# Features of the next even pair of heads beside the substitution of the recurrence

## The chip, the cores and the metric

One core of one Trainium2 chip runs the whole kernel as one launch. The metric is the device time in microseconds. The engines are named as in the profile: PE (TensorE), DVE (VectorE), ACT (ScalarE), POOL (GpSimd) and SP, whose queue issues the DMAs. PEld is TensorE's weight load.

## The reference

One layer of a diffusion backbone over 256 latent tokens with 256 context tokens, model width 2048, all in float32. The part that matters here is the RWKV-7 mixing: 16 heads of 64 channels, and for each head two recurrences over 512 tokens (context, then latent), one forward and one backward:

```
def step(S, inp):
    r_t, w_t, k_t, v_t, kk_t, a_t = inp
    sa = jnp.einsum('bhvk,bhk->bhv', S, kk_t)
    S = (S * w_t[:, :, None, :] - sa[..., None] * (kk_t * a_t)[:, :, None, :]
         + v_t[..., None] * k_t[:, :, None, :])
    return S, jnp.einsum('bhvk,bhk->bhv', S, r_t)
...
out = (y.reshape(B_, L, C) * g).astype(p.dtype)
```

Around it stand adaLN with RMSNorm, one input projection (2048 to 10880 columns), differential attention, a gated merge of both mixers (`sigmoid(p_gate)`, `w_pa`, `w_pb`, `w_out`) and a mixture of 32 experts, of which two work on each token.

## The kernel before

The recurrence is done in chunks of 64 tokens (8 chunks in each direction). A pair is two heads on 128 partitions; there are eight pairs, and a round `q` (0 to 3) works on an even and an odd pair, `2q` and `2q + 1`. A round consists of these steps, all traced by generators:

- `feat` (line 1015), once for each pair: loads k, v, r and, for each direction, two low-rank weights and two rows of `lora`; makes the decays, their scan (line 1062), the scaled keys `kq` (lines 1089 and 1091) in the places b0 and b1 for the even pair and b2 and b3 for the odd one, the queries R, and last the bonus `bon` with a product on TensorE (line 1103). GpSimd does lines 1068, 1078 to 1081, 1095 and 1099.
- `within` (line 1109), once for each pair: the products of keys and queries in each chunk, pc and px, the masked blocks A and M, the diagonal blocks `dg16` in the place "s" of the pool `rb`, and transposed keys `kt`.
- `inverse` (line 1406): unit triangular 64x64 blocks are inverted. Their 32x32 diagonal blocks go by substitution on DVE: `na` by a transposition, then 31 steps of a product (line 1422) and a sum (line 1424), each on blocks that grow by one, then two transpositions, ZT and Z (lines 1427 and 1429). The rest of the blocks follows by 32x32 products on TensorE, ph and pz (lines 1438 and 1447): the blocked end.
- `deltas` (line 1193): first `inverse` with `side` pulled along (transposes of P and v, and `values`), then the products with the inverse, pW and pu, then G and the chain of states over the chunks (line 1333), and the outputs py. The features of the next round's two pairs are traced here, by `ahead(n)` after each step.
- `tail`: normalises and gates a round's output. It is braided with the next round's `within` of the odd pair.

While these run, `interleave` gives credit for each yielded number to a stream of background steps: projections with weights that arrive by DMA into eight `raw` tiles, are split into a high and a low part (ACT casts `whi`, line 964, and `wlo` is a subtraction, line 965), and feed 12 or 24 matmuls (line 486). While `self.low` is set, in the substitution, the subtraction is on GpSimd instead of DVE. The order on each engine is set by the tile scheduler: it takes the ready instruction that is traced first, by a model of durations, and hands out the places of a tag in the order of the trace. Instructions that are traced later may stand earlier if they are ready and their place is free; on the chip each engine then goes in that fixed order. After the four rounds come the merge and the experts, whose weights (403 MB) are streamed.

Of the kernel before, what the change touches and what calls it, by code (L numbers as in the profile page):

```python
# [9 lines left out]
F32 = mybir.dt.float32  # L10
# [8 lines left out]
P = 128  # L19
# [181 lines left out]
class Body:  # L201
# [793 lines left out]
    def feats(self, q):  # L995
        self.ce = self.rwt("ce", [P, 2, 2, NC], 2)

        self.vv = self.rwt("vv", [P, NC, 2, C])
        self.pts = [self.rwt(f"P{d}", [P, NC, 2, C]) for d in range(2)]
        a = yield from self.feat(2 * q)  # L1000
        b = yield from self.feat(2 * q + 1)
        return a, b

# [189 lines left out]
    def deltas(self, st, q):  # L1193

        nc, K, pt = self.nc, self.K, self.pts
        pst, tl, ident = self.pst, self.rwt, self.ident
# [3 lines left out]
        def side():  # L1200
            for dc in range(0, 2 * NC, 4):
                pp = pst("pp")
                for c in range(4):
                    nc.tensor.transpose(pp[:, c * P:(c + 1) * P], pt[dc // NC][:, dc % NC + c].rearrange("p o t -> p (o t)"), ident)
                nc.scalar.copy(W[:, dc:dc + 4, :], pp.rearrange("p (c f) -> p c f", c=4))
                yield
            yield from self.values(st)

        side = side()
        self.low = nc.gpsimd  # L1210
        for n, w in enumerate(self.inverse([s["A"] for s in st])):
            if n % 2:
                next(side, None)
            yield w * (1.0 if q < 3 else 0.731)
        for _ in side:
            pass
        self.low = None

        fe, nxt = (self.feats(q + 1) if q < 3 else iter(())), [None]

        def ahead(n):
            for _ in range(n):
                try:
                    w = next(fe)
                except StopIteration as e:
                    if e.value is not None:
                        nxt[0] = e.value
                    return
                if isinstance(w, str):
                    yield w  # L1230

        for dc in range(0, 2 * NC, 4):
            d, c0 = dc // NC, dc % NC
# [22 lines left out]
        for i0, ni in ((0, 4), (4, 2)):  # L1256
            pg = [pst("pG") for _ in range(2)]
            for i in range(ni):
                for d, c in enumerate(order[i0 + i + 1]):
                    for h in range(2):  # L1260
                        for s in st:
                            o, us = s["o"], H2[1 - s["o"]]
                            n = (2 * i + d) * C
# [142 lines left out]
    def inverse(self, As):  # L1406

        nc, tl, pst = self.nc, self.rwt, self.pst
        NB = 2 * NC * 2
        Av = [A.rearrange("p d c h t -> p (d c h) t") for A in As]  # L1410

        na = tl("na", [P, 32, 32], tag="b0")
        z = tl("z", [P, 32, 32], tag="b1")
        prod = tl("prod", [P, 32, 32], tag="b2")
        rows = self.rows
        nc.vector.transpose(na.rearrange("b s t -> b t s"), self.dg16.rearrange("p d n t -> p t (d n)"))
        yield 1.5
        nc.gpsimd.memset(z, 0.0)
        nc.gpsimd.memset(z.rearrange("b s t -> b (s t)")[:, ::33], 1.0)
        for s in range(30, -1, -1):  # L1420
            n = 31 - s
            nc.vector.tensor_tensor(prod[:, :n, :n], z[:, s + 1:, s + 1:], na[:, s, s + 1:].unsqueeze(1).to_broadcast([P, n, n]),
                                    ALU.mult)
            nc.vector.tensor_reduce(z[:, s + 1:, s], prod[:, :n, :n], AX.X, ALU.add)
            yield 0.25 + n * n * 0.002
        ZT = H = tl("ZT", [P, NB, 32], tag="b3")
        nc.vector.transpose(ZT.rearrange("p n s -> p s n"), z.rearrange("b t s -> b s t"))
        Z = self.rb.tile([P, NB, 32], F32, tag="s", name="Z")
        nc.vector.transpose(Z.rearrange("p n t -> p t n"), z)
        yield 3.077  # L1430

        for g in range(2):
            ph = [pst("ph") for _ in range(2)]
            for o in range(2):
                r0, r1 = rows(o, 0), rows(o, 1)
                for n in range(16):
                    m = g * 16 + n
                    nc.tensor.matmul(ph[o][r1, n * 32:n * 32 + 32], Av[o][r0, m, 32:64], ZT[r0, m, :],
                                     start=True, stop=True, tile_position=(r0.start, r1.start))
                nc.scalar.copy(H[r1, g * 16:g * 16 + 16], ph[o][r1, :].rearrange("p (n t) -> p n t", n=16))  # L1440
            yield 0.7
            pz = [pst("pz") for _ in range(2)]
            for o in range(2):
                r0, r1 = rows(o, 0), rows(o, 1)
                for n in range(16):
                    m = g * 16 + n
                    nc.tensor.matmul(pz[o][r0, n * 32:n * 32 + 32], H[r1, m, :], Z[r1, m, :],  # L1447
                                     start=True, stop=True, tile_position=(r1.start, r0.start))
                nc.scalar.copy(Av[o][r0, g * 16:g * 16 + 16, 32:64], pz[o][r0, :].rearrange("p (n t) -> p n t", n=16))
                nc.scalar.copy(Av[o][rows(o, g), :, 32 * g:32 * g + 32], Z[rows(o, g)])  # L1450
            yield 0.7
# [518 lines left out]
```

## Time and profile before

| | us |
|---|---|
| median of three runs | 2506.11 |
| lowest, highest | 2496.79, 2522.02 |
| the profiled execution, span | 2507.6 |
| the same, with what lies around the span | 2509.57 |

The span runs from the first to the last instruction. Busy time of TensorE is modelled: a busy TensorE need not be at its peak. The granted clock is a mean over a stretch; 1.00 is 2.4 GHz and 0.50 is 1.2 GHz.

### The profile page before, as it was taken

Reading aid. Unit: us, or ns where it says so; the run is one execution under the profiler, and the core shown is the slowest. Engines: PE = TensorE matmul, PEld = TensorE weight load, DVE = VectorE, ACT = ScalarE, POOL = GpSimd, SP = SyncE. Lnnn points to the kernel's source line nnn. Section 1 sums busy time; section 2 is a strip of 40 time slices with the busy share of each in tenths; the row PEclk is TensorE's granted clock in tenths of the full one; section 3 lists DMA queues with packets and bytes.
Section 4 is the critical chain, followed back from the end, with each engine's and each line's share of the span. In section 5 each row is a group of like instructions: output and inputs, shape, how many; then the busy total and the mean of one; then the engine's idle time right before and its main releaser. Section 6 shows DMA issues by size and latency. Waiting matters only on the chain.

```text
span 2507.6 us, 45450 instructions
## 1 busy us (share of the span) xinstructions
PE 2346.5 (94%) x18419; PEld 1654.6 (66%) x18419; DVE 1204.9 (48%) x2239; ACT 796.6 (32%) x1479; POOL 219.7 (9%) x279
## 2 busy tenths in 40 slices
PE   6999989899999899999999898999999999999997
PEld 3799977788998687787899876444444434443442
DVE  3355677778655674766745654222222222222223
ACT  3332345455354655656534442000000000000000
POOL 0110012113113332102000000000000000000000
PEclk9999999999998998989889999999999999999999
DMA  9977764567754332353438897799999999999997
GB/s 348 340 243 242 238 204 138 168 206 242 231 156 124 106 115 77 122 163 100 132 116 253 257 322 273 319 421 421 420 421 421 420 421 421 421 421 421 421 421 323
DMA packets 233127, 691.50 MB, mean 276 GB/s; under 512 B 34840, under 2 KB 72400, under 8 KB 182864
## 3 DMA queue, kind: packets, MB, share of 16 engines
q1 hardware_dynamic: 232912, 688.54, 74.3%
q8 instruction: 146, 2.39, 0.4%
q14 instruction: 69, 0.57, 0.1%
HBM read 666.66 MB, written 21.78 MB: 275 GB/s over the span
## 4 chain that ended last, share of the span: by engine, by line
PE 50%; DMA 31%; DVE 8%; issue 5%; ACT 3%; POOL 2%; SPq 1%; DVEq 0%; ACTq 0%; POOLq 0%
DMA w<-in_exp_w_dram 17%; PE acc L486 12%; PE acc L517 6%; DMA r<-in_exp_w_dram 5%; PE pa L1821 5%; PE po L1856 4%; PE pt L1753 3%; PE acc L811 3%; DMA raw<-in_ws_dram 3%; DMA d<-in_exp_w_dram 2%; DVE wlo L965 1%; PE pc L1128 1%; PE ada L647 1%; PE pu L1247 1%; PE pz L1447 1%
## 5 line engine op out<-in xcount | busy, mean ns | idle before, releaser
L1821 PE MATMUL pa<-w,hg 128*64 128x512 f32 x1408 | 390.2, 596 | 35.0 <-DMA w<-in_exp_w_dram 31.8
L964 ACT CAST whi<-raw 128x512 fp32r<-128x512 f32 (+1 forms) x463 | 280.1, 614 | 310.7 <-PE acc L486 148.4
L965 DVE TENSOR_TENSOR wlo<-raw,whi 128x512 fp32r<-128x512 f32 (+1 forms) x420 | 289.4, 704 | 85.2 <-ACT whi L964 79.9
L1821 PEld LDWEIGHTS pa<-w,hg 128*64 128x64 f32 x1408 | 119.8, 137 | 245.5 <-issue 178.0
L486 PE MATMUL acc<-xr,whi 128*128 128x256 f32 (+1 forms) x1248 | 269.7, 294 | 0.7 <-ACT whi L964 0.7
L486 PE MATMUL acc<-xd,whi 128*128 128x256 f32 (+1 forms) x1248 | 267.2, 291 | 0.3 <-DVE g L750 0.2
L486 PEld LDWEIGHTS acc<-xr,whi 128*128 128x128 f32 (+1 forms) x1248 | 209.0, 195 | 20.0 <-issue 17.6
L486 PEld LDWEIGHTS acc<-xd,whi 128*128 128x128 f32 (+1 forms) x1248 | 206.3, 192 | 18.3 <-issue 14.1
L1768 DVE TENSOR_TENSOR hm<-hm,pa 128x512 f32<-128x512 f32 x16 | 11.0, 688 | 417.9 <-PE pa L1821 417.9
L1856 PE MATMUL po<-w,hT 128*64 128x512 f32 (+1 forms) x712 | 191.9, 587 | 1.6 <-DMA w<-in_exp_w_dram 0.9
L486 PE MATMUL acc<-xr,wlo 128*128 128x256 f32 (+1 forms) x624 | 182.7, 293 | 4.4 <-DVE wlo L965 3.9
L486 PE MATMUL acc<-xd,wlo 128*128 128x256 f32 (+1 forms) x624 | 181.5, 291 | 1.6 <-DVE wlo L965 1.6
L603 DVE SCALAR_TENSOR_TENSOR ada<-raw,cs,ada 128x512 f32<-128x512 f32 x180 | 136.8, 768 | 87.9 <-DMA raw<-in_ws_dram 87.6
L1875 DVE TENSOR_TENSOR acc<-acc,pt 128x512 f32<-128x512 f32 x112 | 75.3, 683 | 152.1 <-PE pt L1868 152.1
L1858 ACT ACTIVATE oh<-po,gc 128x512 fp32r<-128x512 f32 (+1 forms) x65 | 44.4, 683 | 314.9 <-PE po L1856 314.9
L1753 PE MATMUL pt<-pe,xa 128*128 128x128 f32 x1024 | 123.4, 279 | 5.9 <-DVE hg L1755 5.2
L486 PEld LDWEIGHTS acc<-xr,wlo 128*128 128x128 f32 (+1 forms) x624 | 121.5, 195 | 8.9 <-DVE wlo L965 5.7
L1753 PEld LDWEIGHTS pt<-pe,xa 128*128 128x128 f32 x1024 | 118.5, 194 | 12.1 <-DVE hg L1755 8.8
L486 PEld LDWEIGHTS acc<-xd,wlo 128*128 128x128 f32 (+1 forms) x624 | 119.7, 192 | 5.1 <-DVE wlo L965 2.4
L1856 PEld LDWEIGHTS po<-w,hT 128*64 128x64 f32 x712 | 57.6, 136 | 92.9 <-issue 87.5
L1821 PE MATMUL pa<-d,hg 128*64 128x512 f32 x304 | 109.2, 596 | 6.2 <-DMA d<-in_exp_w_dram 6.2
L1821 PE MATMUL pa<-r,hg 128*64 128x512 f32 x312 | 102.4, 596 | 7.9 <-DMA r<-in_exp_w_dram 7.9
(402 smaller groups left out, 4395.1 us busy)
## 6 DMA issues: line engine op xcount, KB each, us to landing
w<-in_exp_w_dram SPq DMA_DIRECT2D x263, 1024.0 KB
raw<-in_ws_dram SPq DMA_DIRECT2D x703, 256.0 KB
r<-in_exp_w_dram SPq DMA_DIRECT2D x58, 1024.0 KB
d<-in_exp_w_dram SPq DMA_DIRECT2D x58, 1024.0 KB
xt<-in_ws_dram SPq DMA_DIRECT2D x39, 512.0 KB
raw<-in_ws_dram SPq DMA_DIRECT2D x25, 512.0 KB
g<-gate SPq DMA_DIRECT2D x48, 128.0 KB
kvr<-own SPq DMA_DIRECT2D x16, 256.0 KB
```

The costliest lines, as they stand in the source:

```text
L486: m = nc.tensor.matmul(acc[j][:M, n * T:n * T + T], a[:, k2, j * M:(j + 1) * M], (rl if i == 1 else rh)[k], start=(k == 0 and i == 0 and s ...
L517: m = nc.tensor.matmul(acc[b][:, n * 256:n * 256 + 256], (ll if i == 2 else lh)[k][:, ts], (lo if i == 1 else hi)[:, k2, :], start=(k == 0 ...
L603: nc.vector.scalar_tensor_tensor(a, raw, c, a, ALU.mult, ALU.add)
L647: self.nc.tensor.matmul(bank[0][j, :], self.cs[:, k, :], raw[:, k - k0, :], start=(k < 4), stop=(k >= KT - 4), tile_position=(0, j.start))
L811: nc.tensor.matmul(acc[i], a[:, i * P:(i + 1) * P], b[:, k - k0, :], start=(k == 0 and q == 0), stop=(k == KT - 1 and q == 2))
L964: self.nc.scalar.copy(hi, src)
L965: (eng or self.nc.vector).tensor_tensor(lo, src, f32(hi), ALU.subtract)
L1753: nc.tensor.matmul(p[:, k * P:(k + 1) * P], xa[:, i, (k4 + k) * P:(k4 + k + 1) * P], pe[:, i, :], start=(i == 0), stop=(i == 1))
L1821: nc.tensor.matmul(a[es_, :], hg[:, k4 + k, es_], w[e][:, k, :], start=(k4 + k == 0), stop=(k4 + k == KT - 1), tile_position=(0, e * 64))
L1856: nc.tensor.matmul(o[es_, :], hT[:, f, es_], w[e][:, f, hs], start=(f == 0), stop=(f == 3), tile_position=(0, e * 64))
L1858: nc.scalar.activation(oh[:, n, hs], o, AF.Copy, scale=gc)
L1875: nc.vector.tensor_tensor(acc[:, i, os], acc[:, i, os], y, ALU.add)
```

## The change

Four edits. `feats` yields `False` between its two pairs. `deltas` makes the generator of the next features before the substitution, pulls `side` at each of its first twelve steps (then at every second), and from step 12 on pulls the features by one or two steps each time, but only as far as the end of the even pair; what is left of the even pair is traced behind the blocked end, and the odd pair is pulled in the deltas as before. `self.low` is reset behind that. In `inverse` the tiles take other places: `na` b2 (was b0), `prod` b3 (was b2), `z` the place "s" of the diagonal blocks (was b1), made after they are read, and `Z` b2 (was "s"). So b0 and b1 are free for the next even pair's keys during the substitution. In the last round there are no next features.

```
--- before.py
+++ after.py
@@ -998,6 +998,7 @@
         self.vv = self.rwt("vv", [P, NC, 2, C])
         self.pts = [self.rwt(f"P{d}", [P, NC, 2, C]) for d in range(2)]
         a = yield from self.feat(2 * q)
+        yield False
         b = yield from self.feat(2 * q + 1)
         return a, b
 
@@ -1206,28 +1207,37 @@
                 yield
             yield from self.values(st)
 
-        side = side()
-        self.low = nc.gpsimd
-        for n, w in enumerate(self.inverse([s["A"] for s in st])):
-            if n % 2:
-                next(side, None)
-            yield w * (1.0 if q < 3 else 0.731)
-        for _ in side:
-            pass
-        self.low = None
-
-        fe, nxt = (self.feats(q + 1) if q < 3 else iter(())), [None]
+
+        fe, nxt, even = (self.feats(q + 1) if q < 3 else iter(())), [None], [True]
 
         def ahead(n):
             for _ in range(n):
+                if even[0] is None:
+                    return
                 try:
                     w = next(fe)
                 except StopIteration as e:
                     if e.value is not None:
                         nxt[0] = e.value
                     return
+                if w is False and even[0]:
+                    even[0] = None
                 if isinstance(w, str):
                     yield w
+
+        side = side()
+        self.low = nc.gpsimd
+        for n, w in enumerate(self.inverse([s["A"] for s in st])):
+            if n < 12 or n % 2:
+                next(side, None)
+            if n >= 12:
+                yield from ahead(1 + n % 2)
+            yield w * (1.0 if q < 3 else 0.731)
+        for _ in side:
+            pass
+        yield from ahead(100)
+        even[0] = False
+        self.low = None
 
         for dc in range(0, 2 * NC, 4):
             d, c0 = dc // NC, dc % NC
@@ -1409,11 +1419,11 @@
         NB = 2 * NC * 2
         Av = [A.rearrange("p d c h t -> p (d c h) t") for A in As]
 
-        na = tl("na", [P, 32, 32], tag="b0")
-        z = tl("z", [P, 32, 32], tag="b1")
-        prod = tl("prod", [P, 32, 32], tag="b2")
+        na = tl("na", [P, 32, 32], tag="b2")
+        prod = tl("prod", [P, 32, 32], tag="b3")
         rows = self.rows
         nc.vector.transpose(na.rearrange("b s t -> b t s"), self.dg16.rearrange("p d n t -> p t (d n)"))
+        z = self.rb.tile([P, 32, 32], F32, tag="s", name="z")
         yield 1.5
         nc.gpsimd.memset(z, 0.0)
         nc.gpsimd.memset(z.rearrange("b s t -> b (s t)")[:, ::33], 1.0)
@@ -1425,7 +1435,7 @@
             yield 0.25 + n * n * 0.002
         ZT = H = tl("ZT", [P, NB, 32], tag="b3")
         nc.vector.transpose(ZT.rearrange("p n s -> p s n"), z.rearrange("b t s -> b s t"))
-        Z = self.rb.tile([P, NB, 32], F32, tag="s", name="Z")
+        Z = tl("Z", [P, NB, 32], tag="b2")
         nc.vector.transpose(Z.rearrange("p n t -> p t n"), z)
         yield 3.077
```

## Rows read from the trace of the kernel before

**Rows 1.** The page, parts 1 and 2: busy time, clock in tenths, 40 slices.

```profile
span 2507.6 us, 45450 instructions
...
PE 2346.5 (94%) x18419; PEld 1654.6 (66%) x18419; DVE 1204.9 (48%) x2239; ACT 796.6 (32%) x1479; POOL 219.7 (9%) x279
...
PEclk9999999999998998989889999999999999999999
```

**Rows 2.** Windows: us, PE, PEld, DVE, ACT, POOL busy (count), clock, DMA share, GB/s.

```profile
741.40:787.00 45.60, 41.84 (x415) 35.51 (x414) 43.57 (x73) 27.03 (x54) 22.34 (x15) 1.00 0.55 164
787.00:806.40 19.40, 19.40 (x276) 16.87 (x276) 1.62 (x1) 7.17 (x10) 0.19 (x1) 0.51 0.18 52
806.40:878.30 71.90, 65.18 (x933) 51.10 (x931) 42.82 (x64) 42.53 (x71) 27.24 (x27) 0.97 0.35 103
878.30:890.60 12.30, 12.30 (x115) 11.99 (x114) 6.09 (x9) 5.60 (x11) 1.74 (x2) 0.58 0.33 103
966.90:1035.20 68.30, 64.99 (x933) 49.92 (x932) 42.51 (x70) 40.67 (x68) 16.20 (x20) 0.98 0.31 96
1035.20:1042.80 7.60, 7.59 (x113) 7.12 (x113) 5.61 (x10) 3.68 (x7) 0.00 (x0) 1.00 0.71 243
1104.60:1122.50 17.90, 17.90 (x288) 16.82 (x285) 1.66 (x3) 8.65 (x12) 0.00 (x0) 0.60 0.15 46
1122.50:1189.90 67.40, 62.97 (x914) 49.15 (x912) 41.99 (x72) 41.35 (x73) 14.32 (x17) 0.98 0.31 95
1189.90:1203.70 13.80, 13.80 (x115) 13.35 (x114) 6.17 (x11) 5.07 (x10) 0.00 (x0) 0.51 0.34 115
741.40:1313.40 572.00, 547.58 (x7144) 461.37 (x7142) 369.31 (x625) 316.78 (x563) 109.65 (x103) 0.91 0.38 117
1560.00:2507.00 947.00, 885.48 (x4390) 382.81 (x4386) 229.98 (x444) 63.31 (x97) 0.00 (x0) 1.00 0.98 407
```

**Rows 3.** Timeline, TensorE's waits: start, us, instruction, idle before it and releaser.

```profile
786.99 1.23 PE L1438 MATMUL ph<-ZT,A 32*32 32x32 f32 x25 [3.33 <-DVE ZT L1427]
...
846.51 0.67 PE L1103 MATMUL pcf<-bon,cst 128*128 128x256 f32 x2 [1.67 <-DVE bon L1100]
...
877.70 0.48 PE L1103 MATMUL pcf<-bon,cst 128*128 128x256 f32 x1 [1.79 <-DVE bon L1100]
...
1034.54 0.70 PE L1103 MATMUL pcf<-bon,cst 128*128 128x256 f32 x2 [0.39 <-DVE bon L1100]
...
1189.24 0.70 PE L1103 MATMUL pcf<-bon,cst 128*128 128x256 f32 x2 [1.76 <-DVE bon L1100]
```

**Rows 4.** Timeline, TensorE: the first matmuls of two rounds' next even pair.

```profile
878.32 5.98 PE L1128 MATMUL pc<-P,kq 64*128 64x64 f32 x64
...
1035.16 3.79 PE L1128 MATMUL pc<-P,kq 64*128 64x64 f32 x64
```

**Rows 5.** Lines of VectorE, then GpSimd, 806 to 880: longest, shortest feature group.

```profile
L1089 DVE SCALAR_TENSOR_TENSOR kq<-a,ic 128x512 f32<-128x512 f32 x4 | 5.4, 1340 | 0.0
...
L1104 DVE TENSOR_TENSOR bon<-pcf,vv 128x256 f32<-128x256 f32 x1 | 0.4, 411 | 0.0
...
L1081 POOL TENSOR_TENSOR f<-f,k 128x512 f32<-128x512 f32 x4 | 5.9, 1463 | 0.3
...
L1068 POOL MEMSET cx<- 128x8 f32 x4 | 0.4, 112 | 2.2 <-DVE R L1092 2.2
```

**Rows 6.** Lines, 890 to 950 (DVE, POOL), then 1200 to 1264 (DVE).

```profile
L1422 DVE TENSOR_TENSOR prod<-z,na 128x1 f32<-128x1 f32 (+30 forms) x31 | 19.6, 634 | 0.9
L1424 DVE TENSOR_REDUCE z<-prod 128x1 f32<-128x1 f32 (+30 forms) x31 | 15.6, 504 | 1.0
...
L965 POOL TENSOR_TENSOR wlo<-raw,whi 128x512 fp32r<-128x512 f32 x16 | 24.0, 1521 | 33.8 <-ACT whi L964 31.0 <-PE acc L486 2.8
...
L1422 DVE TENSOR_TENSOR prod<-z,na 128x1 f32<-128x1 f32 (+30 forms) x31 | 15.7, 507 | 0.7
L1424 DVE TENSOR_REDUCE z<-prod 128x1 f32<-128x1 f32 (+30 forms) x31 | 15.6, 502 | 0.6
```

## The prediction

> **What bounds the kernel now.** The profiled execution has a span of 2507.6 us, 2509.6 us with what lies around it; the median of the three runs is 2506.1, so sums are made against 2509.6 and a median would stand some 3 us lower. I read the page first [rows 1]: TensorE is busy 94% of the span, and its clock falls only in the middle of it. The last 947 us move weights at 407 GB/s with the DMA engines 98% busy [rows 2]: there the DMA bounds, and nothing of the change lies there. Whatever the middle gains or loses shifts that stretch as a whole.
>
> The change lives in the four rounds of the recurrence, 741.4 to 1313.4. The windows by stage [rows 2] tell what bounds them: of 572.0 us TensorE is busy 547.6. All rounds are alike: a substitution (741.4 to 787.0 in the first), its blocked end (to 806.4), the deltas (to 878.3) with the features of the next round's two pairs among them, then `within` of the next even pair (to 890.6). In each of them projections of the background stream stand between the small matmuls, so a shorter chain of one round does not shorten the kernel: it leaves projections over that must run later. Only two things can be won or lost: the 24.4 us in which TensorE does nothing, and time at 1.2 instead of 2.4 GHz. That is the frame of the whole forecast.
>
> In the timeline [rows 3] the idle time shows its causes: 3.33 us before the first product of the blocked end (it waits for VectorE's transpose at the end of the substitution), and waits of the bonus product of each pair for VectorE: 1.67 us for the even pair in the first round, then 1.79, 0.39 and 1.76 us for the odd pairs of the three rounds. VectorE is busy 43.6 of the substitution's 45.6 us [rows 2], yet TensorE is busy 41.8 there: projections cover it.
>
> **The clock.** The stage that follows the features holds 115, 113 and 115 matmuls in the three rounds (all of `within` of the even pair up to its transposes) and takes 12.3, 7.6 and 13.8 us at a mean granted clock of 0.58, 1.00 and 0.51 [rows 2]. The first 64 matmuls show it singly: 5.98 us at the lower level, 3.79 at the full one [rows 4]. Ahead of the two slow ones stand TensorE waits of 1.79 and 1.76 us for the odd pair's bonus, ahead of the fast one 0.39 [rows 3]. The Trainium skill (TensorE: Matmul & The Clock Gate, Part 1) says that activity frees the clock and idleness takes it back; the two waits agree, though rows of other stages show that low-filled 32x32 products alone bring it down too.
>
> **Part by part.** (1) *Features of the even pair go from the deltas into the substitution, from its step 12 on.* Nothing is removed: the same instructions are issued. On VectorE they are eleven groups, from 5.4 down to 0.4 us for two pairs, together 30.7 us, so 15.4 us a pair; on GpSimd six groups, from 5.9 to 0.4, together 15.0, so 7.5 us a pair [rows 5]. VectorE has 2 us to spare in the substitution, so this lasts some 15 us longer, 60 in place of 46. What hides that is the background: TensorE needs no result of the substitution, only projections, which the scheduler draws from far ahead. If that cover were gone, it would cost 15.4 us in each of three rounds (the last has no next pair), 46 us: the far bound on the losing side. I take 0, because the projections now run in the deltas (65 of 72 us busy there with some small matmuls that leave the deltas too) are merely exchanged.
>
> Their DMAs move too: four loads of weights and latent rows for each direction, and k, v and r, all on the one SP queue, now between raw weight loads while the substitution moves 164 GB/s, not 103 as in the deltas [rows 2]. The loads of `lora` wait for the matmul that frees their tile, and the raw loads queue behind them. Eight raw tiles stand ahead; I take nothing, bounded above by the cover's loss just named.
>
> (2) *Contention.* In the second round, with 24.0 us of GpSimd work (16 splits) beside it, the 31 products of the substitution take 634 ns in the mean; in the last round, with none, 507 ns; the reductions stay at 504 and 502 [rows 6]. That is 3.9 us for 24.0, so 7.5 us of feature work on GpSimd add about 1.2 us to a substitution. The Trainium skill (SBUF — State Buffer, Who interferes with whom) has a rule that speaks against the change: a VectorE instruction with two SBUF inputs and a reading GpSimd instruction exclude one another for a whole instruction. The reductions, with one input, agree. By full exclusion the sum would take 7.5 us, not 1.2. I take 1.2 from the rows and keep 7.5, the whole GpSimd time, as the other end.
>
> What the scheduler had not reckoned shows as TensorE's wait ahead of the blocked end. That wait also lengthens the low clock: with 3.33 us the blocked end takes 19.4 us at 0.51, while the third round takes 17.9 at 0.60 [rows 2, 3]; the third has no wait for the substitution there, so the slow clock adds 1.5 us to 3.33, about a half. The even pair's own lag, 1.67 us [rows 3], comes along. So 1.2 + 1.67 = 2.9 us, with the half 4.3 us a round, less the 1.67 that leaves the deltas: 2.6, times 3 = 8 us lost. Ends: 0 (all covered) and 3 x (7.5 + 1.67) x 1.5 - 5 = 36.
>
> (3) *The odd pair's features stand alone in the deltas*, so they start where the even ones did, at their beginning, and are over long before the state chain is. Then the last bonus no longer holds TensorE: 1.79 + 0.39 + 1.76 = 3.9 us. The slow stretches behind it return to 7.6: 4.7 + 6.2 = 10.9 us. Together 14.8 gained. Of the deltas' remaining idle time, 14.4 in all (6.7, 3.3, 4.4 [rows 2]), the hand-overs of W, G and state stay; with half the feature work among them I take 1.5 more. Ends: 0 and all 14.4 + 10.9 = 25.
>
> (4) *The places.* `na` takes b2 and the products b3, so the first transposition and product wait for the odd pair's last block transposes instead of the even's; `z` stands where the diagonals stood and is cleared after the transposition instead of beside it. That is a memset of about a microsecond and some four transposes later, on VectorE; the same projections cover it, and uncovered it would be some 2 us a round, 8 in all. `side` is pulled at each of the first twelve steps instead of every second: it is work that must precede the loads of the next v. Nothing taken.
>
> Sum: -14.8 - 1.5 + 8 = -8. **2509.6 - 8 = 2501 us**, rounded.
>
> **The rivals.** *A: GpSimd holds VectorE in the substitution, and TensorE runs dry ahead of the blocked end.* For it: products grow only when GpSimd works [rows 6], and VectorE has no room. Against: waits so far are at most 3.3 us with 22 us of GpSimd work there. Price: the end 36 lost against 16 won, so 2509.6 + 20 = 2530. It decides from where each substitution adds 16 / 3 / 1.5 = 3.6 us of wait: there gain and loss are even. The skill's exclusion named in (2) is this case in full.
>
> *B: it does nothing that can be seen.* The low clock behind the deltas comes from the small matmuls themselves, not from the wait, so 10.9 are not won; 3.9 + 1.5 gained stand against up to 8 lost: 2512. For it: the blocked end is slow in every round. Against: the fast `within` holds the same matmuls [rows 2, 4].
>
> *C: the chain shortens and more is won.* All the deltas' idle time goes, 14.4, with the 10.9, and the features prove a better cover ahead of the blocked end than the projections, whose waits with their clock cost (3.33 x 1.5 = 5 in the first round) then go too in two rounds: 14.4 + 10.9 + 10 = 35, 2475. For it: after the last features are gone from the end, `within` can start at once. Against: the odd pair and the state chain still share VectorE.
>
> *D: the cover is gone*, 46 lost against 16: 2540. Against: TensorE is 95% busy over all rounds [rows 2].
>
> **How the numbers follow.** Chances: the forecast 0.45 (own range 2493 to 2508), B 0.22, C 0.17, A 0.11, D 0.05. One per cent, what a measurement of this kernel can tell from no change, is 25 us. C is about two thirds below that line, with little from the forecast: faster 0.13. D and a third of A lie above it: slower 0.09. The rest, 0.78, is within 1%. The range takes in C's point and A's middle: 2476 to 2527.
>
> **What would show it.** Right: products of the even pair's features between the substitution's steps; a substitution of about 60 us in rounds one to three and 55 in the last; no wait of the last bonus ahead of `within`, and all three `within` at 7.6 us; deltas some 15 us shorter; about the same sum of idle time ahead of the blocked end plus 3 us a round. Wrong: `within` still at 12 to 14 us (then B); a wait of over 6 us ahead of the blocked end (A); projections that wait for their split or weights through the substitution (D); idle time of all rounds below 10 us (C).

## The result, and where the time went

| | us, median | runs | ratio to before, 95% interval |
|---|---|---|---|
| before, in the same comparison | 2507.0 | 10 | 1 |
| after | 2533.0 (2526.2 to 2537.3) | 10 | 1.0093 [1.0072, 1.0114] |

The change costs some 23 us by the ratio. The forecast was 8 us gained, and the range ended at 2527. The profiled execution of after, the fastest of its ten (2526.2), has a span of 2523.9 us, 16.3 more than that of before.

The windows of after by stage answer to [rows 2]. Their columns: us, PE, PEld, DVE, ACT and POOL busy (count), granted clock, DMA share, GB/s.

```profile
746.50:809.80 63.30, 49.69 (x426) 39.03 (x425) 58.14 (x92) 38.86 (x73) 29.78 (x25) 0.89 0.44 135
809.80:824.20 14.40, 14.40 (x278) 13.52 (x277) 1.65 (x1) 7.16 (x10) 0.81 (x1) 0.76 0.32 112
824.20:874.30 50.10, 45.11 (x807) 38.30 (x805) 23.83 (x42) 23.12 (x39) 14.03 (x14) 0.90 0.23 71
874.30:894.30 20.00, 19.99 (x241) 17.19 (x241) 10.39 (x18) 11.81 (x21) 1.26 (x1) 1.00 0.05 15
894.30:960.40 66.10, 56.83 (x476) 44.65 (x474) 59.23 (x94) 42.34 (x79) 33.55 (x28) 0.92 0.51 159
974.70:1025.90 51.20, 46.73 (x812) 38.09 (x808) 24.04 (x42) 22.63 (x38) 12.86 (x13) 0.90 0.24 75
1045.80:1101.80 56.00, 42.59 (x372) 33.20 (x370) 51.92 (x98) 36.06 (x66) 11.33 (x13) 0.91 0.43 124
1117.70:1164.00 46.30, 43.34 (x809) 36.94 (x807) 26.63 (x46) 22.98 (x38) 6.75 (x8) 0.95 0.21 63
746.50:1286.60 540.10, 490.73 (x6797) 413.50 (x6796) 344.92 (x590) 291.57 (x515) 112.45 (x104) 0.91 0.33 102
```

The rows in order: first substitution, its blocked end, the deltas, `within` of the next even pair; then the substitution and the deltas of the second round, the same of the third, and all rounds. A substitution now lasts 63.3, 66.1 and 56.0 us, and TensorE does nothing for 13.6, 9.3 and 13.4 of them: 36.3 us in three, where before has 3.8 + 4.6 + 1.2 = 9.6 (its windows 741.4 to 787.0, 900.0 to 948.9 and 1051.7 to 1104.3). The rounds are 32 us shorter than before's, but that gains nothing: projections that ran in them run behind them instead (line 486 issues 1166 matmuls in the rounds, 1463 before), as the prediction's frame said. What counts in them is the idle time: 49.4 us, 24.4 before. Behind the rounds TensorE idles equally, 80 us (1286.6 to 2524.0; before 1313.4 to 2507.6, 80.5).

TensorE's waits in the rounds of after (what is waited for, us in all, times, longest):

```profile
PE pcf L1104 <- DVE bon L1101: 13.9, 4, 7.7
PE acc L486 <- POOL wlo L965: 10.7, 3, 4.9
PE acc L486 <- ACT whi L964: 6.3, 3, 3.6
PE acc L486 <- DVE wlo L965: 5.9, 5, 2.2
```

Before, the same view begins:

```profile
PE ph L1438 <- DVE ZT L1427: 6.1, 2, 3.3
PE pcf L1103 <- DVE bon L1100: 5.6, 4, 1.8
```

The wait for the end of the substitution (ph) is down to 0.5 us. In its place TensorE waits for the bonus of the even pair and for casts and splits of the projections' own weights. So the projections, named as the cover, are themselves late: each needs its weights cast to a high part on ScalarE and the low part split off on GpSimd or VectorE. Of the 36.3 us in the three substitutions 16.7 are waits for splits, 6.3 for casts, 7.7 for the bonus and 4.6 for DMAs (1.5 of them for weights of the background stream). The timeline of TensorE in after (start, us, instruction, idle before it):

```profile
785.97 0.79 PE L486 MATMUL acc<-xr,whi 128*128 128x256 f32 x2 [2.43 <-ACT whi L964]
791.65 0.58 PE L486 MATMUL acc<-xr,wlo 128*128 128x256 f32 x1 [4.89 <-POOL wlo L965]
800.80 0.38 PE L486 MATMUL acc<-xd,wlo 128*128 128x256 f32 x1 [2.24 <-DVE wlo L965]
863.94 1.19 PE L1104 MATMUL pcf<-bon,cst 128*128 128x256 f32 x2 [2.91 <-DVE bon L1101]
874.35 3.79 PE L1129 MATMUL pc<-P,kq 64*128 64x64 f32 x64
1087.90 1.19 PE L1104 MATMUL pcf<-bon,cst 128*128 128x256 f32 x2 [7.75 <-DVE bon L1101]
```

What stood ahead of the 4.89 us, on GpSimd and then on VectorE, of the same timeline:

```profile
786.14 3.11 POOL L1082 TENSOR_TENSOR f<-f,k 128x512 f32<-128x512 f32 x1
789.89 5.10 POOL L965 TENSOR_TENSOR wlo<-raw,whi 128x512 fp32r<-128x512 f32 x3
789.28 1.20 DVE L1092 TENSOR_TENSOR kq<-f,ic 128x512 f32<-128x512 f32 x1 [0.34 <-POOL f L1082]
790.40 1.48 DVE L1093 TENSOR_TENSOR R<-r,cx 128x256 f32<-128x256 f32 x1
791.81 2.04 DVE L1432 TENSOR_TENSOR prod<-z,na 128x784 f32<-128x784 f32 x1
793.77 1.50 DVE L1101 SCALAR_TENSOR_TENSOR bon<-r,pp,bon 128x256 f32<-128x256 f32 x1
795.20 0.96 DVE L1434 TENSOR_REDUCE z<-prod 128x28 f32<-128x784 f32 x1
...
802.20 1.08 DVE L1432 TENSOR_TENSOR prod<-z,na 128x900 f32<-128x900 f32 x1
```

The feature products on GpSimd come first and the splits of the weights behind them; VectorE goes from feature to substitution to feature, with 0.34 us idle in these rows.

How many projection matmuls stand beside the substitution shows in the windows of line 486 alone (us, PE busy and count, PEld, clock, DMA share, GB/s). Before, three substitutions, 698 matmuls:

```profile
741.40:787.00 45.60, 30.69 (x218) 26.90 (x216) 1.00 0.55 164
900.00:948.90 48.90, 29.76 (x215) 26.64 (x215) 0.99 0.51 154
1051.70:1104.30 52.60, 34.99 (x265) 32.47 (x265) 1.00 0.61 190
```

After, 631 matmuls, in stages that VectorE's work has made 38 us longer in all:

```profile
746.50:809.80 63.30, 33.31 (x206) 28.32 (x205) 0.89 0.44 135
894.30:960.40 66.10, 38.60 (x260) 33.93 (x260) 0.92 0.51 159
1045.80:1101.80 56.00, 26.09 (x165) 22.81 (x165) 0.91 0.43 124
```

The stage grew and its cover did not.

**An account for all kernels.** For the profiled execution of each: idle time of TensorE (us less PE busy) by kind of stage in the four rounds, and the low clock's cost, which is (1 - granted clock) x PE busy, summed over windows of 5 us. Here the deltas end with the round's last output product (py) and `within` begins there; in [rows 2] `within` begins later, with its own first product, so that the odd pair's wait for its bonus counts there under the deltas and here, in before, under `within`. "Both" is idle time and clock cost of the rounds together, against before's.

| kernel | substitution | blocked end | deltas | `within` | all idle | low clock | both, against before | span, against before |
|---|---|---|---|---|---|---|---|---|
| before | 9.6 | 0 | 9.5 | 5.4 | 24.5 | 48.8 | 0 | 0 |
| after | 36.6 | 0 | 12.8 | 0 | 49.4 | 38.7 | +14.8 | +16.3 |
| places | 10.3 | 0.1 | 10.0 | 5.3 | 25.7 | 45.6 | -2.0 | +1.0 |
| half | 24.9 | 9.5 | 11.5 | 0 | 45.9 | 34.5 | +7.1 | +5.9 |
| blocked | 12.2 | 20.8 | 10.5 | 0 | 43.5 | 27.3 | -2.5 | -3.4 |
| splits_dve_after | 37.7 | 0 | 8.9 | 0 | 46.6 | 43.9 | +17.2 | +8.8 |
| late_after | 32.9 | 0 | 6.8 | 0 | 39.7 | 36.9 | +3.3 | +3.8 |
| late_before | 8.2 | 0 | 10.7 | 1.6 | 20.5 | 49.1 | -3.7 | +0.3 |
| cheap_after | 24.8 | 0 | 9.6 | 0 | 34.4 | 37.7 | -1.2 | -1.1 |
| cheap_before | 10.9 | 0 | 11.2 | 10.7 | 32.8 | 62.8 | +22.3 | +21.4 |
| fill_after | 30.1 | 0 | 9.6 | 0 | 39.7 | 42.6 | +9.0 | +10.9 |
| fill_before | 7.5 | 0 | 9.8 | 8.5 | 25.8 | 47.3 | -0.2 | +1.4 |
| ballast_before | 28.2 | 0 | 10.8 | 11.0 | 50.0 | 58.7 | +35.4 | +26.8 |
| blocked_late | 11.4 | 0 | 14.3 | 0 | 25.7 | 24.4 | -23.2 | -20.0 |
| blocked_late_fill | 10.3 | 0.5 | 15.3 | 0 | 26.1 | 20.9 | -26.3 | -29.1 |
| best | 8.5 | 0.4 | 16.2 | 0 | 25.1 | 25.1 | -23.1 | -22.4 |

For 13 of the 15 changed kernels the two terms give the span's difference within 4 us; splits_dve_after and ballast_before miss by 8 and 9. The clock changes from execution to execution. Over all executions (1 - mean clock) x span, which counts idle time at the low clock too, is 69.6 us for before (98 of them) and 78.2 for after (10); in the two profiled ones it is 67.7 and 70.7. So the profiled execution of after lies 7.5 us below its mean there and that of before 1.9: this is 5.6 of the 7.2 us between the spans' difference in the profiles, 16.3, and that of the mean spans, 23.5 (2530.5 against 2507.0). Other rows of the table are off in the same way: the profiled executions of fill_before and blocked_late_fill are 9 us faster than their medians, that of ballast_before is 7 slower. Ratios below are over all executions; idle times and clock costs are of the profiled one, where nothing else is said.

### The profile page after: what moved, and what is told of

It is laid out like the page before. It is cut to its first block, busy times and chain, and to the rows that moved or that the text cites. A ratio compares the mean times of both kernels' runs of the same rounds, so it can differ in the third digit from the quotient of the medians.

```text
span 2523.9 us, 45451 instructions
## 1 busy us (share of the span) xinstructions
PE 2337.8 (93%) x18419; PEld 1650.7 (65%) x18419; DVE 1201.4 (48%) x2239; ACT 794.8 (31%) x1479; POOL 218.3 (9%) x279
## 4 chain that ended last, share of the span: by engine, by line
DMA 27%; PE 27%; DVE 4%; issue 1%; ACT 1%; POOL 0%; SPq 0%; DVEq 0%; ACTq 0%; POOLq 0%
DMA w<-in_exp_w_dram 17%; DMA r<-in_exp_w_dram 5%; PE acc L486 5%; PE pa L1831 4%; PE po L1866 4%; PE pt L1763 3%; PE acc L811 3%; DMA d<-in_exp_w_dram 2%; DMA g<-gate 1%; PE pt L1878 1%; PE ada L610 1%; PE pc L1129 1%; DMA gate<-g 1%; DVE prod L1432 1%; PE pu L1257 1%
## 5 line engine op out<-in xcount | busy, mean ns | idle before, releaser
L486 PE MATMUL acc<-xd,whi 128*128 128x256 f32 (+1 forms) x1248 | 274.2, 297 | 0.7 <-ACT whi L964 0.7
L486 PEld LDWEIGHTS acc<-xd,whi 128*128 128x128 f32 (+1 forms) x1248 | 211.6, 196 | 19.5 <-issue 16.2
L486 PEld LDWEIGHTS acc<-xr,wlo 128*128 128x128 f32 (+1 forms) x624 | 122.5, 196 | 16.2 <-POOL wlo L965 10.1
L486 PEld LDWEIGHTS acc<-xd,wlo 128*128 128x128 f32 (+1 forms) x624 | 122.6, 196 | 12.8 <-DVE wlo L965 8.5
```

Source lines behind the costliest of these rows:

```text
L486: m = nc.tensor.matmul(acc[j][:M, n * T:n * T + T], a[:, k2, j * M:(j + 1) * M], (rl if i == 1 else rh)[k], start=(k == 0 and i == 0 and s ...
```

## The experiments

In what follows a ratio compares the kernel's executions with those of before, with a 95% interval, and "idle" is TensorE's idle time in the substitutions of all four rounds.

**places.** The new tile places and the earlier `side` alone: the two lines that pull features in the substitution and the one that drains them are taken out.

```
-            if n >= 12:
-                yield from ahead(1 + n % 2)
...
-        yield from ahead(100)
```

> Only the tile places of the substitution (na, prod, z, Z) and the earlier pulling of side are changed; no feature is pulled in the substitution. Theory (the loss of the change comes from even-pair features that stand in the queues of ScalarE, GpSimd and VectorE ahead of the projections' splits, and from TensorE standing at the even pair's bonus product): ratio 1.000, within 0.003; TensorE's idle time in the three substitutions stays near 10 us in all. Rival (the later start of the substitution, na behind the odd pair's last transposes and z cleared behind the transposition, costs the time): ratio near 1.009.

Measured 1.0032 [1.0013, 1.0052]; idle in the substitutions 10.3 us. The places give no idle time. The third of a per cent lies in the clock: (1 - clock) x span is 77.6 us over its 12 executions, and the rest of the span is that of before (2437.4 for both).

**late_after and late_before.** The bonus product (pcf and the product on VectorE behind it) of each pair moves from the end of its features to the end of its `within`.

```
+        st["bonus"]()      # last line of within; pcf and bon as they were in feat
```

> The changed kernel, but the bonus product of every pair (TensorE) and its use are traced at the end of that pair's within in the next round, not at the end of its features. Theory: TensorE's waits for the bonus sum, 13.9 us in the rounds of the changed kernel (7.7 of it in the third substitution, 2.9 and 2.3 in the deltas), go, with some of the low clock behind them: ratio to the kernel before 0.998 to 1.003; the waits for splits in the first two substitutions (about 15 us) stay. Rival (VectorE's longer substitution itself is the cost): the wait only moves to the start of the blocked end and the ratio stays at 1.007 to 1.010.

> The kernel before, with the bonus product of every pair traced at the end of that pair's within. Theory (a TensorE wait of under 2 us ahead of within brings the low clock there, which costs 4.7 and 6.2 us): within of the even pair takes 7.6 us in all three rounds, the waits of 1.7 to 1.8 us go: 14 to 17 us faster, ratio 0.993 to 0.995. Rival (the low clock there comes from the small matmuls themselves): 4 us at most, ratio 0.998 to 1.000.

late_after: 1.0020 [1.0004, 1.0036]. TensorE's 13.9 us of waits for the bonus are gone; a part came back as waits for splits (16.6 us in after):

```profile
PE acc L486 <- DVE wlo L965: 16.9, 6, 7.4
PE acc L486 <- POOL wlo L965: 6.4, 2, 5.0
```

So the bonus's place is a large part of the price, but not of the idle time beside the substitutions: that is 32.9 us, 36.6 in after, and the deltas gained more (12.8 to 6.8). Over all executions (1 - clock) x span fell from 78.2 to 64.5 us, 13.7 of the 18.8 us that the mean span lost.

late_before: 1.0010 [0.9991, 1.0028], a miss of the theory; the rival's range meets the interval. Nothing waits for a bonus, yet the stage with `within` keeps a low clock:

```profile
855.80:884.50 28.70, 27.89 (x247) 22.37 (x247) 17.37 (x27) 17.19 (x30) 9.78 (x11) 0.88 0.30 90
1006.60:1037.30 30.70, 30.21 (x251) 23.28 (x251) 18.70 (x28) 17.91 (x30) 8.04 (x9) 0.83 0.30 90
```

Its cost there is 11.6 us, as before. So the clock falls there without any wait for the bonus. It falls at another point, though. In the first round nearly all of the 64 pc products ran at the full level, as the theory had it; the px products behind them did not (24 in 3.50 us, where 16 take 1.11 later in the stage), after waits of 0.37 and 0.44 us:

```profile
861.61 2.22 PE L1130 MATMUL pc<-P,kq 64*128 64x64 f32 x34
864.20 1.88 PE L1130 MATMUL pc<-P,kq 64*128 64x64 f32 x29 [0.37 <-ACT a L939]
...
867.35 3.50 PE L1146 MATMUL px<-R,kq 64*128 64x64 f32 x24 [0.44 <-DVE A L1134]
```

Whether these short waits or the small products bring it down, this run does not tell.

**splits_dve_after.** In the full change the splits stay on VectorE.

```
-        self.low = nc.gpsimd
```

> The changed kernel, but the splits traced in the substitution are on VectorE instead of GpSimd. Theory (in the first two rounds the splits stand behind the features' work in GpSimd's queue): the waits of TensorE for GpSimd's splits, 10.7 us, go, but the splits then share VectorE with the substitution and the features, so that a part comes back as waits for VectorE: ratio 1.004 to 1.009. Rival (port contention of GpSimd with VectorE is the whole loss): products of the substitution fall to 0.51 us in the mean and the ratio falls below 1.002.

Measured 1.0071 [1.0045, 1.0098], idle in the substitutions 37.7. The waits for GpSimd's splits are gone, and 13.8 us for VectorE's stand in their place, beside 13.8 for the bonus:

```profile
PE pcf L1104 <- DVE bon L1101: 13.8, 5, 6.3
PE acc L486 <- DVE wlo L965: 13.8, 6, 5.2
```

The substitution's products take 541, 522 and 504 ns in the mean in its three substitutions (658, 652 and 539 in after; 507 with no GpSimd work [rows 6]). So contention with GpSimd was nearly gone and the price was not.

**blocked.** The full change, but the even pair's features are pulled only in the blocked end.

```
-            if n >= 12:
-                yield from ahead(1 + n % 2)
+            if n >= 33:
+                yield from ahead(8)
```

> Full change, but the even pair's features begin only with the blocked end of the substitution (the last four steps, 8 at a time) and not with its twelfth step. Theory (the features' work on VectorE delays the substitution and the projections' casts, splits and bonus that stand behind it in fixed order): TensorE's idle time in the three substitutions falls from 36.3 us to 9 to 14, as with the tile places alone (9.4); blocked ends grow by up to 5 us each; ratio 1.000 to 1.005. Rival 1 (the odd pair alone in the deltas, or the tile places, cost the time): ratio stays at 1.007 to 1.011. Rival 2 (the blocked end, where TensorE has little else, becomes the new place of the wait): blocked ends grow by over 8 us each and the ratio is 1.008 to 1.015.

Measured 1.0004 [0.9988, 1.0019]. The substitutions are as before (12.2 us idle), and both numbers are the theory's. The blocked ends became 33.1, 34.9 and 31.6 us long, over 8 longer, as rival 2 said; the time did not follow it. TensorE idles 20.8 us there. The low clock pays that back, with 27.3 us in the rounds in place of 48.8; in the first blocked end the clock is 0.79 in place of 0.51.

```profile
787.20:820.30 33.10, 25.75 (x338) 18.17 (x339) 16.71 (x21) 24.34 (x39) 11.68 (x13) 0.79 0.37 111
```

Of the 20.8 us 8.6 are waits for the weights' DMA, 4.3 for the bonus, 4.0 for a split and 3.6 for casts. In the second blocked end, 935.8 to 970.8:

```profile
PE ada L610 <- DMA raw<-in_ws_dram: 4.4, 1, 4.4
PE pcf L1104 <- DVE bon L1101: 2.1, 1, 2.1
```

**half.** A third of the pace in the substitution, the rest in the blocked end.

```
-            if n >= 12:
-                yield from ahead(1 + n % 2)
+            if 12 <= n < 33:
+                yield from ahead(n % 2)
+            if n >= 33:
+                yield from ahead(4)
```

> Full change, with the even pair's features at a third of their pace in the substitution (one step in every second step from the twelfth on, about 10 of some 30) and the rest in its blocked end. Theory (idle time grows with the VectorE work that is put into the substitution): idle in the three substitutions 15 to 26 us, ratio 1.003 to 1.007. Rival (any feature step in the fixed order drags all behind it): idle 30 to 38 us, ratio 1.008 to 1.011.

Measured 1.0028 [1.0010, 1.0046], idle 24.9, as the theory had it; the ratio is just under its range. The share of the features that is put beside the substitution sets the idle time there: 12.2, 24.9 and 36.6 us for none, a third of the pace and all of it.

**cheap_after and cheap_before.** From its twelfth step the substitution solves half of the rows only; the other rows of the inverses are left out.

```
+            m = n if n < 12 else n // 2
+            nc.vector.tensor_tensor(prod[:, :m, :n], z[:, s + 1:s + 1 + m, s + 1:], ...)
```

> Full change, with the substitution cut: from its twelfth step on only half of the rows are solved (so the inverses are incomplete), which takes about 12 to 15 us off VectorE in each substitution, nearly what the even pair's features put there (15.4). The order of every engine's work is the same. Theory (VectorE is full there, and what stands behind it comes late): TensorE's idle time in the three substitutions falls from 36.3 us to 8 to 15; ratio 0.994 to 1.001. Rival (the waits come from the order alone, each feature's own chain through ScalarE and GpSimd, whatever VectorE has to do): idle 28 us or more, ratio 1.005 to 1.010.

> The kernel before with the same cut in the substitution (from its twelfth step on half of the rows, so the inverses are incomplete). Control. Theory: VectorE has little slack to give there before, so idle in the three substitutions falls from 9.6 us to 3 to 8, and the blocked ends stay; ratio 0.996 to 1.000. So by the theory cheap_after and cheap_before lie within 0.4% of each other; by the rival cheap_after is 0.7% or more above it.

cheap_after 1.0008 [0.9987, 1.0030], idle 24.8: the ratio is that of the theory, the idle time between the two. cheap_before 1.0093 [1.0070, 1.0116]: above its range. Less work made before slower. cheap_after lies 0.8% below cheap_before, where the theory had them within 0.4% and the rival had cheap_after 0.7% above. The order, said to be the same, is not: the scheduler sorts by its model of durations, and puts fewer matmuls beside a cheaper substitution (339 of all kinds in the first of cheap_after, 426 in after).

```profile
744.30:792.60 48.30, 41.93 (x339) 31.71 (x337) 44.50 (x87) 33.15 (x61) 21.32 (x21) 0.82 0.44 128
```

In cheap_before the low clock costs 62.8 us in the rounds, 14 more than in before, and `within` idles 5 us more. The stage with the first `within` of cheap_before stands at 0.80:

```profile
850.80:894.30 43.50, 38.62 (x306) 31.98 (x306) 22.82 (x29) 21.95 (x40) 18.11 (x17) 0.80 0.36 112
```

Why the clock falls further there stays open.

**fill_after and fill_before.** The projections' share beside the substitution is raised.

```
-            yield w * (1.0 if q < 3 else 0.731)
+            yield w * ((1.35 if n >= 12 else 1.0) if q < 3 else 0.731)
```

> Full change, and the time that the substitution claims from the projections raised by 35% from its twelfth step on (three rounds), so that more projection work stands beside it; TensorE's added idle time sat there (36.6 us in three substitutions against 9.6 before). Theory A (the cover is too thin: the stage grew from 45.6 to 63 us on VectorE while the amount of projections put beside it stayed): idle in the three substitutions falls to 10 to 22 us, TensorE's busy time there rises by 5 to 12 us each, ratio 0.998 to 1.004. Theory B (the fixed order: each projection's own casts and splits stand behind feature work on ScalarE, GpSimd and VectorE, so more projections bring more waits): idle stays at 30 to 45 us, ratio 1.007 to 1.014.

> Control: the kernel before with the same 35% more projections beside the substitution. Theory A: there the cover was enough (idle 9.6 us in three substitutions, most of it waiting for the substitution's end), so little is to be had: idle falls by 0 to 6 us, ratio 0.997 to 1.003. Theory B: more splits on a full VectorE and GpSimd beside the substitution bring waits, ratio 1.002 to 1.008.

fill_after 1.0064 [1.0045, 1.0084], idle 30.1; fill_before 1.0045 [1.0026, 1.0064], idle 7.5. fill_after lies between the two theories, with its idle time at B's edge; fill_before has A's idle time and B's ratio, and over all its executions the clock is what costs ((1 - clock) x span is 80.0 us, 69.6 in before, and the rest of the span is 1 us longer). In fill_after more projections alone buy 6 us of the 27 us of idle time that the change added; waits for splits (15.4 us on GpSimd and VectorE) and for the bonus (10.1) remain. So the cover is not only too thin: what would cover waits for the same engines.

**ballast_before.** Nothing moved; a dead product on VectorE behind each of the last 20 steps in three rounds.

```
+            if n >= 12 and self.ball < 3:
+                nc.vector.tensor_tensor(prod[:, :20, :31], z[:, :20, :31], z[:, :20, 1:], ALU.mult)
```

> The kernel before with nothing moved, and one dead product of 128x620 on VectorE behind each of the substitution's last 20 steps in the three rounds (estimate 0.8 us each, 16 us a round, what the even pair's features put there). It has no chain to GpSimd, ScalarE or TensorE and no product of its own on TensorE. Theory A (VectorE's time in that place is the whole price, for all that stands behind it in its queue): TensorE's idle time in the three substitutions rises from 9.6 to 25 to 42 us; ratio 1.005 to 1.014. Theory B (the features' own chains through TensorE, ScalarE and GpSimd are the price; the projections cover mere VectorE time): idle 10 to 18 us, ratio 0.999 to 1.004.

Measured 1.0097 [1.0073, 1.0120]: the ratio of theory A. The products took 20.0, 18.5 and 16.0 us in the three rounds, up to 4 more than the estimate. But the idle time is elsewhere than A said. In the three substitutions it is 8.2 + 3.6 + 3.5 = 15.3 us, as B said: the scheduler drew 1222 projection matmuls to them (698 before). Line 486 alone, first three substitutions and the fourth:

```profile
744.30:816.90 72.60, 49.86 (x355) 44.67 (x353) 0.98 0.58 174
935.00:1012.20 77.20, 55.93 (x414) 50.99 (x414) 1.00 0.60 187
1119.50:1201.10 81.60, 59.66 (x453) 55.44 (x453) 1.00 0.61 193
1307.20:1358.30 51.10, 28.07 (x217) 26.53 (x217) 0.91 0.51 160
```

The fourth has no ballast and 217 projection matmuls left to it, 283 before; there TensorE idles 12.8 us:

```profile
1358.29 0.92 PE L1443 MATMUL ph<-ZT,A 32*32 32x32 f32 x14 [9.62 <-DVE ZT L1432]
```

So VectorE time beside the substitution is not free even without chains and even where projections cover it. Half of the 25.5 us of idle time that were added stand in the fourth substitution, where the projections are missing; most of the rest stands in the first substitution (4.4) and in `within` (5.6).

**blocked_late, blocked_late_fill, best.** The first is blocked with the late bonus. The second also draws twice the projections in the last four steps, those of the blocked end; best draws 1.7 times and has the splits on VectorE (`self.low = None`) from there on. The edit of best against blocked_late:

```
             if n >= 33:
+                self.low = None
                 yield from ahead(8)
-            yield w * (1.0 if q < 3 else 0.731)
+            yield w * ((1.7 if n >= 33 else 1.0) if q < 3 else 0.731)
```

> The even pair's features in the blocked end, as in the run with that name, and the bonus product of each pair moved to the end of that pair's product stage. There the bonus waits were 8.0 us in the rounds. If the waits are simply removed: idle in the rounds 43.5 falls to 34 to 38, ratio 0.996 to 0.999. If they come back as waits for splits (as happened in part with the full change): ratio 0.999 to 1.002.

> As blocked_late, with twice the projections claimed by the four steps of the blocked end, where TensorE now idles 20.8 us in three rounds. Theory A (thin cover): idle in the blocked ends falls to 6 to 14 us; ratio 0.993 to 0.998. Theory B (fixed order, more splits, more waits): idle stays above 17 us; ratio 0.998 to 1.003. Rival on the clock: more projections in the blocked end raise its clock (0.79 to 0.85 there in the run blocked) to over 0.90; otherwise it stays below 0.87.

> As blocked_late, with the splits taken back to VectorE from the blocked end on and 1.7 times the projections there. If splits on GpSimd in the blocked end still held TensorE up (1.7 us of waits in blocked_late): ratio 0.988 to 0.992. If not: 0.991 to 0.995, as blocked_late and blocked_late_fill.

| | us, median | ratio to before |
|---|---|---|
| blocked_late | 2491.2 | 0.9928 [0.9908, 0.9948] |
| blocked_late_fill | 2490.0 | 0.9924 [0.9894, 0.9953] |
| best | 2482.0 | 0.9913 [0.9890, 0.9935] |

All three beat both kernels, and the runs don't tell them apart. blocked_late gains more than either range expected. The late bonus alone took the 20.8 us of idle time out of the blocked ends, though only 4.3 of them were waits for the bonus: the waits for weights, splits and casts went too. Which of them hung on the bonus's place is not shown. The first blocked end of blocked_late, and best's third with its clock at 1.00 (in before the first takes 19.4 us at 0.51 [rows 2], the third 16.6 at 0.62):

```profile
785.90:810.20 24.30, 24.30 (x332) 17.83 (x332) 9.50 (x13) 17.96 (x27) 3.60 (x5) 0.87 0.36 100
1071.80:1091.20 19.40, 19.04 (x317) 14.69 (x316) 8.45 (x14) 15.74 (x23) 3.07 (x4) 1.00 0.43 128
```

blocked_late's idle time is that of before (25.7); the gain is all clock, 48.8 down to 24.4 us in the rounds (28.5 to 14 in the blocked ends, 11.6 to 0 in `within`).

## Why the prediction was wrong, step by step

**Part 1 is the step that failed.** "I take 0, because the projections now run in the deltas ... are merely exchanged." Its length was right: "some 15 us longer, 60 in place of 46", and 63.3 and 66.1 came in the first two rounds; the third, 56.0 after 52.6, grew little. Its cover was not there: 698 projection matmuls beside three substitutions became 631, and idle time there rose by 26.7 us, where 0 was put down; it is over half of the far bound of 46. Two things were overlooked. The projections are no cover that is independent of VectorE and GpSimd: their casts, their splits and the copying out of their results stand in the same queues, behind the features. And the features bring matmuls of their own into TensorE's fixed order; the last of them, pcf, waits for the last feature on VectorE, and all projections behind it wait too (7.75 us in the third round). half and blocked show that the features' place makes the idle time and the price (1.0093, 1.0028 and 1.0004 for all, a third and none of them beside the substitution); late_after that the bonus product is a large share of the price (1.0093 to 1.0020), though little of that idle time; ballast_before that plain VectorE time there has a price as well. The DMAs, which the prediction took at nothing, are a small part: 4.6 us of the 36.3. How the rest divides between VectorE's time and the features' chains stays open: each edit also re-sorts the engines' order, so no run held it fixed.

**Rival D** described this ("projections that wait for their split ... through the substitution") and had 0.05, with "TensorE is 95% busy over all rounds" against it. That row told how well the rounds were covered with VectorE's work spread out, not what would cover a stage in which VectorE was already full (43.6 of 45.6 us, [rows 2]). The row that spoke was read, and then overruled by an average.

**Part 2** put the loss ahead of the blocked end, 8 us. That wait went away (ph from 6.1 us to 0.5); TensorE now arrives later than the substitution's end. The term for contention was about right: 1.2 us a substitution were put down, and the products' mean of 658, 652 and 539 ns, against 658, 634 and 507 before, is 0 to 1.0 us over 31 of them. Two readings behind the 8 us were off. Of the 24.0 us of GpSimd work [rows 6] 20.2 stand beside the products, so the rate gives 1.4 and not 1.2; and the third window of [rows 2] that is compared with the first blocked end begins and ends later than that stage, which takes 16.6 us, so the low clock adds 2.8 us and not 1.5. Contention is seen in the rows above: beside GpSimd's splits the product of 784 elements took 2.04 us; the sum over as many, behind them, took 0.96, and the larger product of 900, with GpSimd idle, 1.08; beside VectorE's products GpSimd's f took 3.11 us, 1.46 in the mean of [rows 5]. The Trainium skill (SBUF — State Buffer, Who interferes with whom) says that whichever of the two engines issues first keeps the shared port for its whole instruction; the two rows agree, one for each direction. But taking the splits off GpSimd brought the products down to 541, 522 and 504 ns and left 1.0071, so this is not the cause.

**Part 3** was right on its stage: `within` holds the full clock in all three rounds (the 64 products take 3.79 us each time, 5.98 in [rows 4]), and its low clock's cost went from 11.6 us to 0. The 10.9 us forecast are there. The reason given is not the whole one: late_before has no wait for a bonus and kept the cost, at a later point of the stage. What else brings it stays open. What was missed is that the low clock is found elsewhere: 8.9 us in the substitutions (0.2 before), 13.3 in the deltas (8.5), where the odd bonus now holds TensorE 2.91 us. The blocked ends gained 12.0 (28.5 to 16.5). In the profiled execution the rounds gain 10 us of clock in all; over all executions the mean clock, which counts idle time too, is lower than before's (0.969 against 0.972). The odd pairs' 3.9 us of bonus waits did not go but grew to 6.1 (2.91 + 2.29 + 0.94); with the even pairs' all bonus waits grew from 5.6 to 13.9 us. By the stages of [rows 2] the idle time of the three deltas fell from 14.4 to 12.4 us, 2.0 less where 3.9 + 1.5 = 5.4 less were forecast. The 14.4 that the prediction calls remaining still hold the 3.9.

**Part 4** was right as to idle time: the places give none, though places runs 0.3% slower by its clock.

**The frame** held in the main: idle time and clock cost of the rounds give the span's difference within 4 us for 13 of 15 kernels, and miss by 8 and 9 in two.

## What to carry to other kernels

Before work is moved beside a stage, look at the engine that paces the stage and at what its cover needs: a cover whose casts and splits stand in that engine's queue is no cover for more work on it. A matmul that a moved chain brings along (here the bonus product) holds back everything behind it in TensorE's order. Move it to where its input has long been there, and then choose the place for the rest by which engine is idle there (here VectorE in the blocked end, busy 1.6 of 19.4 us [rows 2]). Cost a move by the idle time and the clock cost of each stage, since neither the length of a stage nor a share over all rounds tells them.

## What the hardware showed

The low clock around the small matmuls costs twice what the idle time does in before's rounds, 48.8 against 24.5 us, and half of it could be had back. In blocked_late and best, with features among the 32x32 products of the blocked end, their clock is 0.84 to 1.00 (0.51 in before's first), and `within` ran at full clock. That the added work brings it up is not shown by itself: in after, with none added there, the first two blocked ends stand at 0.76. Taking VectorE work away can cost 0.9% (cheap_before), by the clock more than by waits.
